# The RWKV-7 recurrence of a two-layer encoder: its products issued chunk by chunk in one fixed order, and the dense operands moved to multiples of 128 bytes

## Chip, cores and metric

The kernel runs on 1 core of one Trainium2 chip. The metric is the time of one execution on the device in microseconds (us). For the kernel before, three runs are shown; the profile is of one further execution, which the hardware profiler recorded.

## What is computed

The reference is an encoder trunk of two layers over 1024 positions of width 1024, all in float32. Layer 0 mixes positions with a gated block and trailing means, layer 1 with RWKV-7; a SwiGLU feed-forward network (FFN) with 2816 hidden units follows each. The part that the change rewrites is the recurrence of layer 1, for 16 heads of size 64:

```python
def step(state, inp):
    r_t, w_t, k_t, v_t, a_t, b_t = inp
    sa = jnp.einsum('bhvk,bhk->bhv', state, a_t)
    state = (state * w_t[:, :, None, :] + sa[..., None] * b_t[:, :, None, :]
             + v_t[..., None] * k_t[:, :, None, :])
    return state, jnp.einsum('bhvk,bhk->bhv', state, r_t)

s0 = jnp.zeros((bsz, nh, n, n), jnp.float32)
_, ys = lax.scan(step, s0, xs)
```

Around it stand plain matrix products: `h @ w` for the mixers' projections and `(silu(hn @ w_gate) * (hn @ w_up)) @ w_down` for the FFN.

## The kernel before

**Dense products.** The sequence is worked in two halves of 512 positions (`h` = 0 and 1). Each operand of a dense product is split into a high and a low part in the type float32r (`split`, L126: a copy on ACT, a subtraction on DVE), and each product is three matmuls, high times high, high times low and low times high (`mm3`, L323 to L326), with a stationary block of 128 by 128 weights and a moving block of 128 by 512 activations. The built program has 9,152 matmuls with float32r operands, 9,120 of them on the full 128 by 128 array. Weights come by DMA on ACT's queue, three tiles ahead, in the order of a list that is written out beforehand (`push...`, `take`).

**Recurrence.** `recur(h, wp)` (L1125) turns each half into 8 chunks of 64 positions, 16 chunks in all. All of its products are plain float32 and small, and each runs on a part of the array: 64 by 64 tiles for the Gram products (L1175, into `gt`), the chunk's own part (L1221), the product with the state (L1144, `sm<-S,ar`), the solve (L1144, `sm<-Q,XT`) and the output from the old state (L1266); 128 by 64 for the new state (L1250) and the output from the chunk (L1275); 32 by 32 for the two products that complete the triangular inverse (L1191 and L1210); the full array for the transposes (L1203, and L1330 in `post`). In a trace each of these matmuls is two instructions. `prep(c)` loads a chunk (SP's queue) and makes everything that doesn't need the state; `chain(c)` carries the state: product with the state, `Q` on DVE (L1237), solve, `uv` on ACT and DVE (L1241, L1242), new state, two DVE operations (L1256, L1257), and the outputs `yp`; `post` normalizes two chunks and stores them. PSUM has three buffers `sm` for all of these products, three `mm` for the dense ones and one for `yp`.

**What sets the order.** `recur` is a generator that yields a cost after each group of products. `drive` (L712) runs an FFN generator, which yields after every 3 matmuls (an eighth of a unit), and steps `recur` beside it until the costs that it yielded make up `RATIO` = 3.0 times the FFN's units. Every step of `recur` is emitted at a priority raised by `AHEAD` = 300, and a scheduler then places the instructions of each engine. It may interleave the products of different groups, and does. The two recurrences stand beside the FFN of layer 0 (second half) and of layer 1 (first half), L1473 and L1522.

**Tiles.** Pools of tiles are stacked from both ends of the on-chip memory. Several small tiles lie ahead of the large ones, such as `onesd` (one float), `mhalf`, `vec2`, `hfv`, `xss`, `hlast`, `pct`, and their widths set the addresses of what follows.

Of the kernel before, what the change touches and what calls it, by code (L numbers as in the profile page):

```python
# [12 lines left out]
ALU = mybir.AluOpType  # L13
# [16 lines left out]
RATIO, AHEAD, INV, FINE = 3.0, 300, 5, 1  # L30
LOWRANK_AT, GATE_AT, MIX_AT = (5, 8), (7, 8), 2

# [4 lines left out]
def tile_trunk(  # L37
# [11 lines left out]

    def open_pool(**kw):  # L50
        es = ExitStack()
        return es.enter_context(tc.tile_pool(reuse_waits="tile", **kw)), es
# [5 lines left out]
    const = ctx.enter_context(tc.tile_pool(name="const", bufs=1, side="left"))  # L58
    wst = ctx.enter_context(tc.tile_pool(name="wst", bufs=3, side="left"))
# [6 lines left out]
    onesd = const.tile([P, 1], F32, name="onesd")  # L66
    pool.memset(onesd, 1.0 / D)
    mhalf = const.tile([P, 16], F32, name="mhalf")
# [5 lines left out]
    vec2 = const.tile([P, 8], F32, name="vec2")  # L74
    omv = const.tile([P, P], F32, name="omv")
    hfv = const.tile([P, 16], F32, name="hfv")
# [212 lines left out]
    nt = ctx.enter_context(tc.tile_pool(name="nt", bufs=1, side="left"))  # L289
# [58 lines left out]
    def norm_rows(ms, scale=1.0):  # L348

        rs = nt.tile([P, 4], F32, tag="nrs", bufs=2, name="nrs")  # L350
# [56 lines left out]
    xss = const.tile([P, 8], F32, name="xss")  # L407
# [334 lines left out]
    hlast = const.tile([P, KT, 1], F32, name="hlast")  # L742
# [44 lines left out]
    def project_gate(h, hn1, kp, xlp, ring):  # L787
# [52 lines left out]
        def side():  # L840
            yield from split_steps()
            yield from mix_steps(hn1, 5, xs, ring_tiles(ring), kp)
            xr = act_tiles(xlp, 1 + HT)
            yield from mix_steps(hn1, 0, keep["xr"], lambda k: [x[:, k, 0:HT] for x in xr], kp)
            yield from mix_steps(hn1, 2, keep["xk"], ring_tiles(ring), kp)
# [279 lines left out]
    def recur(h, wp):  # L1125

        def wt(tag, bufs, shape):
            return wp.tile(shape, F32, tag=tag, bufs=bufs, name=tag)
# [10 lines left out]
        S = [state_d]  # L1139

        def prod(o, lhs, rhs):
            for p in range(8):
                for r in range(2):
                    pe.matmul(o[rows[r], p, :], lhs(r, p), rhs(r, p), start=True, stop=True)  # L1144
                if p == 3:
                    yield 0.7

        def prep(c):
# [18 lines left out]
            yield 0.2  # L1167
            gt = wt("gt", 2, [P, 8, 2, P])
            for q in range(2):
                og = [pst("sm").rearrange("p (a b) -> p a b", b=P) for _ in range(2)]  # L1170
                for j in range(4):
                    p = q * 4 + j
                    for b in range(2):
                        for r in range(2):
                            pe.matmul(  # L1175
                                og[r][rows[b], j, :], bk[rows[r], p, b, :],
                                ar[rows[r], p].rearrange("p a b -> p (a b)"), start=True, stop=True,
                            )
                    if j == 1:
                        yield 0.9  # L1180
                for r in range(2):
                    dve.tensor_tensor(
                        out=gt[:, q * 4 : q * 4 + 4, r, :], in0=og[r], in1=bc(gm.unsqueeze(1), [P, 4, P]), op=ALU.mult
                    )
                yield 0.9

            ow = smt()
            for p in range(8):
                for r in range(2):
                    b0 = r * 64  # L1190
                    pe.matmul(  # L1191
# [6 lines left out]
            yield 0.9  # L1198
            bkt = wt("bkt", 1, [P, 8, P])
            for q in range(2):  # L1200
                o = pst("sm").rearrange("p (a b) -> p a b", b=P)
                for j in range(4):
                    pe.transpose(o[:, j, :], bk[:, q * 4 + j].rearrange("p a b -> p (a b)"), ident)  # L1203
                act.activation(bkt[:, q * 4 : q * 4 + 4, :], o, AF.Copy)  # L1204
                yield 0.5
            ox = smt()
            for p in range(8):
                for r in range(2):
                    b0 = r * 64
                    pe.matmul(  # L1210
# [5 lines left out]
            yield 0.9  # L1216

            ov = smt()
            for p in range(8):
                for r in range(2):  # L1220
                    pe.matmul(  # L1221
                        ov[rows[r], p, :], gt[rows[1 - r], p, r, 0:64], uv[rows[1 - r], p, r, :], start=True, stop=True
                    )
                if p == 3:
                    yield 0.7
            akv = wt("akv", 1, [P, 8, 64])
            act.activation(akv, ov, AF.Copy)
            C[c] = (ar, uv, gt, bkt, XT, akv)
            yield 0.7

        def chain(c):
            ar, uv, gt, bkt, XT, akv = C.pop(c)
            S0 = S[0]
# [4 lines left out]
            yield 0.7  # L1238
            ou = smt()
            yield from prod(ou, lambda r, p: XT[rows[r], p, :], lambda r, p: Q[rows[r], p, :])  # L1240
            act.activation(uv[rows[0], :, 0, :], ou[rows[0]], AF.Copy)  # L1241
            dve.tensor_copy(uv[rows[1], :, 1, :], ou[rows[1]])  # L1242
            yield 0.7
            cg = h * 8 + c
            if cg < NCH - 1:
                Sn = state_d if c == 7 else wt("S", 2, [P, 8, 64])
                os_ = smt()
                for p in range(8):
                    for r in range(2):
                        pe.matmul(  # L1250
                            os_[rows[r], p, :], bkt[:, p, r * 64 : r * 64 + 64], uv[:, p, r, :], start=True, stop=True
                        )
# [317 lines left out]
```

## Time and profile before

| | us |
|---|---|
| median of the three runs (2617.55 to 2632.25) | 2624.68 |
| the profiled execution, its own time | 2628.69 |
| its span, from first to last instruction | 2627.0 |
| mean granted TensorE clock in it | 0.979 |

PE is the engine of the matmuls (TensorE), PEld its weight loads, DVE, ACT and POOL the vector, scalar and GpSimd engines, SP the engine that issues most of the transfers. A matmul's row in the trace shows when it started and a modelled duration. Matmuls overlap, so the distance from start to start, here called the pitch, says what one of them costs. PEclk is the share of the TensorE clock that was granted.

### The profile page before, as it was taken

To read this page: it belongs to the slowest core of one execution; us is meant where nothing else is said; L and a number is where in the kernel's file an instruction comes from. 1 tells how busy PE (TensorE), PEld (TensorE's weight loads), DVE (VectorE), ACT (ScalarE), POOL (GpSimd) and SP (SyncE) were. 2 spreads that over 40 slices of the span, in tenths; PEclk is the share of its full clock that TensorE was granted. 3 is DMA by queue.
4 is the path that set the end of the run, shared out by engine and by line. 5 is a ranking of instruction groups with operands and counts; after the bars stand their busy time and mean duration, and the time that the engine had idled before them with its cause. 6 is when DMAs were issued, how large, how long until landed. Compare 5 with 4: busy or idle time off the path is not lost.

```text
span 2627.0 us, 37918 instructions
## 1 busy us (share of the span) xinstructions
PE 2552.5 (97%) x15735; PEld 2041.2 (78%) x15735; DVE 1403.4 (53%) x2118; ACT 892.0 (34%) x1335; POOL 300.1 (11%) x298
## 2 busy tenths in 40 slices
PE   8999999999989999999999899999999999999998
PEld 6788888888767778788877677777877778888887
DVE  5446544345956864455547846754445454534344
ACT  6233332233543432232324644332133323423223
POOL 0200000001223300011002323201011000100001
PEclk9999999999989999999999999989999999999999
DMA  5113343232364683443233465683443332423321
GB/s 173 48 59 94 120 139 102 73 120 93 96 178 121 160 240 98 115 132 104 78 113 129 134 165 127 175 225 86 106 136 97 121 112 80 145 76 110 103 88 57
DMA packets 434956, 310.69 MB, mean 118 GB/s; under 512 B 93216, under 2 KB 395424, under 8 KB 433760
## 3 DMA queue, kind: packets, MB, share of 16 engines
q10 hardware_dynamic: 297280, 210.53, 27.1%
q1 hardware_dynamic: 137504, 97.75, 13.4%
q8 instruction: 123, 2.02, 0.3%
q14 instruction: 49, 0.40, 0.1%
HBM read 254.68 MB, written 53.54 MB: 117 GB/s over the span
## 4 chain that ended last, share of the span: by engine, by line
PE 85%; DVE 7%; DMA 4%; issue 2%; ACT 1%; POOL 0%; ACTq 0%; SPq 0%; DVEq 0%; POOLq 0%
PE mm L324 22%; PE mm L325 22%; PE mm L326 22%; PE sm L1175 2%; PE sm L1221 1%; PE sm L1144 1%; DVE wlo L128 1%; PE sm L1203 1%; DVE mix L868 1%; PE sm L1210 1%; PE sm L1191 1%; PE yp L1266 1%; PE yp L1275 1%; PE sm L1250 1%; DMA raw<-y_d 1%
## 5 line engine op out<-in xcount | busy, mean ns | idle before, releaser
L325 PE MATMUL mm<-alo,whi 128*128 128x512 f32 x1952 | 783.3, 401 | 1.6 <-DVE alo L128 1.6
L324 PE MATMUL mm<-ahi,whi 128*128 128x512 f32 x1952 | 778.6, 400 | 6.1 <-DVE h L403 5.1
L326 PE MATMUL mm<-ahi,wlo 128*128 128x512 f32 x1952 | 774.3, 397 | 2.5 <-DVE wlo L128 2.5
L127 ACT ACTIVATE whi<-raw 128x1024 fp32r<-128x1024 f32 x288 | 303.9, 1056 | 781.9 <-PE mm L325 647.6
L128 DVE TENSOR_TENSOR wlo<-raw,whi 128x1024 fp32r<-128x1024 f32 x288 | 362.6, 1259 | 308.6 <-ACT whi L127 291.8
L324 PEld LDWEIGHTS mm<-ahi,whi 128*128 128x128 f32 x1952 | 370.7, 190 | 99.5 <-ACT xhi L872 4.3
L326 PEld LDWEIGHTS mm<-ahi,wlo 128*128 128x128 f32 x1952 | 370.2, 190 | 89.2 <-DVE wlo L128 3.4
L325 PEld LDWEIGHTS mm<-alo,whi 128*128 128x128 f32 x1952 | 370.1, 190 | 87.6 <-DVE alo L128 3.2
L324 PE MATMUL mm<-hidhi,wdhi 128*128 128x512 f32 x624 | 241.0, 395 | 5.9 <-ACT hidhi L652 4.2
L325 PE MATMUL mm<-hidlo,wdhi 128*128 128x512 f32 x624 | 244.7, 392 | 1.1 <-DVE hidlo L653 1.0
L326 PE MATMUL mm<-hidhi,wdlo 128*128 128x512 f32 x624 | 244.9, 392 | 0.0
L403 DVE TENSOR_TENSOR h<-h,mm 128x512 f32<-128x512 f32 x192 | 129.4, 686 | 181.1 <-PE mm L326 180.4
L127 ACT ACTIVATE wdhi<-raw 128x1024 fp32r<-128x1024 f32 x82 | 86.5, 1061 | 236.9 <-DMA raw<-in_ffn_w_down_dram 145.7
L649 DVE TENSOR_TENSOR sg<-sg,mm 128x512 f32<-128x512 f32 x88 | 60.3, 687 | 183.3 <-PE mm L326 182.8
L128 DVE TENSOR_TENSOR wdlo<-raw,wdhi 128x1024 fp32r<-128x1024 f32 x82 | 102.8, 1255 | 91.9 <-ACT wdhi L127 91.9
L324 PEld LDWEIGHTS mm<-hidhi,wdhi 128*128 128x128 f32 x624 | 117.1, 188 | 34.4 <-ACT hidhi L652 5.5
L325 PEld LDWEIGHTS mm<-hidlo,wdhi 128*128 128x128 f32 x624 | 117.4, 188 | 26.7 <-DVE hidlo L653 2.4
L326 PEld LDWEIGHTS mm<-hidhi,wdlo 128*128 128x128 f32 x624 | 117.4, 188 | 25.0 <-issue 0.2
L403 DVE TENSOR_TENSOR hA<-hA,mm 128x512 f32<-128x512 f32 x72 | 48.9, 686 | 74.5 <-PE mm L326 74.5
L329 POOL TENSOR_TENSOR nrs<-nrs,mhalf 128x4 f32<-128x4 f32 x8 | 10.0, 1245 | 614.2 <-DVE nrs L351 614.2
L324 PE MATMUL mm<-xhi,whi 128*128 128x512 f32 (+1 forms) x160 | 66.0, 413 | 4.2 <-ACT k L906 4.2
L1204 ACT ACTIVATE bkt<-sm 128x512 f32<-128x512 f32 x32 | 19.1, 597 | 138.1 <-PE sm L1203 121.5
(298 smaller groups left out, 3162.8 us busy)
## 6 DMA issues: line engine op xcount, KB each, us to landing
raw<-in_ffn_w_gate_dram ACTq DMA_DIRECT2D x88, 512.0 KB
raw<-in_ffn_w_up_dram ACTq DMA_DIRECT2D x88, 512.0 KB
raw<-in_ffn_w_down_dram ACTq DMA_DIRECT2D x88, 512.0 KB
raw<-in_ab_w_in_dram ACTq DMA_DIRECT2D x16, 512.0 KB
raw<-in_ab_w_out_dram ACTq DMA_DIRECT2D x16, 512.0 KB
raw<-in_rwkv_w_k_dram ACTq DMA_DIRECT2D x16, 512.0 KB
raw<-in_rwkv_w_r_dram ACTq DMA_DIRECT2D x16, 512.0 KB
ar_d<-ar SPq DMA_DIRECT2D x16, 512.0 KB
```

What stands on the lines that cost most here:

```text
L127: act.activation(hi, src, AF.Copy)
L128: (eng or dve).tensor_tensor(out=lo, in0=src, in1=hi.bitcast(F32), op=ALU.subtract)
L324: pe.matmul(o, whi, xhi, start=first, stop=False)
L325: pe.matmul(o, whi, xlo, start=False, stop=False)
L326: pe.matmul(o, wlo, xhi, start=False, stop=last)
L403: dve.tensor_tensor(out=H[h][:, m, :], in0=H[h][:, m, :], in1=o, op=ALU.add)
L649: dve.tensor_tensor(out=s, in0=s, in1=o, op=ALU.mult)
L868: dve.scalar_tensor_tensor(out=t, in0=hn1[:, k, 0:HT], scalar=col(c), in1=t, op0=ALU.mult, op1=ALU.add)
L1144: pe.matmul(o[rows[r], p, :], lhs(r, p), rhs(r, p), start=True, stop=True)
L1175: pe.matmul(og[r][rows[b], j, :], bk[rows[r], p, b, :], ar[rows[r], p].rearrange("p a b -> p (a b)"), start=True, stop=True,)
L1191: pe.matmul(ow[b0 + 32 : b0 + 64, p, 0:32], gt[b0 : b0 + 32, p, r, 32:64], x1[b0 : b0 + 32, p, :], start=True, stop=True, tile_position=(b ...
L1203: pe.transpose(o[:, j, :], bk[:, q * 4 + j].rearrange("p a b -> p (a b)"), ident)
```

## The change

Three things change; what is computed stays the same, and so do the number and the sizes of all matmuls.

1. **The recurrence in bursts.** `prep` and `chain` are replaced by `load`, `gram`, `flip_bk`, `below`, `below2`, `own` and `burst`. Every matmul and transpose of the recurrence goes through `ordered`, which issues it after the one before it, so that their order on PE is the written one, with all products of one tile size in a row. The preparation of chunk `c + 1` (two Gram groups, transposes, first triangular product) stands inside the burst of chunk `c`; its loads are issued one chunk earlier, and `akv` and the second triangular product follow at the start of the next burst. A burst yields 0.1 after each group, and 12 units in two halves after its end, with `post` between them for odd chunks. The output from the old state is moved ahead of the new state.
2. **`AHEAD`** is 450 in place of 300.
3. **Addresses.** `Lines` widens each tile of a dense pool to a multiple of 32 floats (128 bytes); five small tiles become columns of one tile of 64 floats, `hlast` too; the small `nrs` and `fss` move to a pool of their own, on the other side, padded with `rest`; and the split tile of `side` is read as a dense one of 512 columns rather than at a stride of 513.

```diff
-RATIO, AHEAD, INV, FINE = 3.0, 300, 5, 1
+RATIO, AHEAD, INV, FINE = 3.0, 450, 5, 1
...
+BURST = 12.0
...
+        def tile(self, shape, dt, **kw):
+            n = math.prod(shape[1:])
+            if n % 32 == 0:
+                return self.pl.tile(shape, dt, **kw)
+            t = self.pl.tile([shape[0], n + -n % 32], dt, **kw)[:, :n]
...
+    small = const.tile([P, 64], F32, name="small")
+    onesd, mhalf, vec2, hfv, xss = (small[:, a:b] for a, b in ((56, 57), (0, 16), (16, 24), (24, 40), (40, 48)))
...
+    ns = ctx.enter_context(tc.tile_pool(name="ns", bufs=1, side="right"))
+    ns.tile([P, 8], F32, name="rest")
...
+        def ordered(f, *args, **kw):
+            if last:
+                with tc.issue_after(last.pop()):
+                    i = f(*args, **kw)
+            else:
+                i = f(*args, **kw)
+            last.append(i.ins)
...
+        def burst(c, bkt, w1):
+            ar, _, uv, gt, _, XT = C[c]
+            cg, S0, more = h * 8 + c, S[0], c < 7
+            below2(c, w1)
+            akv = own(c)
             oq = smt()
-            yield from prod(oq, lambda r, p: ar[rows[r], p, 0, :], lambda r, p: S0[rows[r], p, :])
+            each(oq, lambda r, p: ar[rows[r], p, 0, :], lambda r, p: S0[rows[r], p, :])
             Q = wt("Q", 1, [P, 8, 64])
             dve.tensor_tensor(out=Q, in0=akv, in1=oq, op=ALU.add)
-            yield 0.7
+            yield 0.1
+            if more:
+                gram(c + 1, 0)
+                yield 0.1
             ou = smt()
...
+            if more:
+                gram(c + 1, 1)
+                yield 0.1
             if cg < NCH - 1:
...
+            if more:
+                bkt = flip_bk(c + 1)
+                if c < 6:
+                    load(c + 2)
+                yield 0.1
+                w1 = below(c + 1)
+                yield 0.1
+            return bkt, w1
...
+        load(0)
+        load(1)
+        yield 0.2
+        gram(0, 0)
+        yield 0.5
+        gram(0, 1)
+        yield 0.5
+        bkt = flip_bk(0)
+        w1 = below(0)
+        yield 2.0
         for c in range(8):
-            yield from chain(c)
-            if c < 7:
-                yield from prep(c + 1)
+            bkt, w1 = yield from burst(c, bkt, w1)
+            yield BURST / 2
             if c % 2 == 1:
                 yield from post(c // 2)
+            yield BURST / 2
```

On PE, before, at the start of one chunk of the first half: the output from the old state (`yp<-S,ar`), the second triangular product (32 by 32, `sm<-XT,w`) and the chunk's own part (`sm<-uv,gt`) stand like this:

```order
L1266 MATMUL yp<-S,ar 64x64 x8
L1210 MATMUL sm<-XT,w_7941 32x32
L1221 MATMUL sm<-uv,gt 64x64 x2
L1210 MATMUL sm<-XT,w_7941 32x32 x10
L1221 MATMUL sm<-uv,gt 64x64
L1210 MATMUL sm<-XT,w_7941 32x32
```

The last two kinds go on in turn, one product of each, eight more rows. On PE, after, the same place in the burst of the second chunk, behind seven dense matmuls (L1168 is the line of `mm`, through which all of them go):

```order
L1168 MATMUL sm<-ar,bk 64x128 x15
L1168 MATMUL sm<-Q,XT 64x64 x16
L1168 MATMUL yp<-S,ar 64x64 x16
L1168 MATMUL sm<-ar,bk 64x128 x16
L1168 MATMUL sm<-uv,bkt 64x64 x16
L1168 MATMUL yp<-uv,gt 64x64 x16
L1168 MATMUL sm<-ident,bk 128x128 x8
L1168 MATMUL sm<-XT,gt 32x32 x16
```

Each group is whole and the groups follow each other without dense matmuls between them. Counted over the two recurrences, neighbours on PE that run on different tile sizes were 580 and are 154; of these, changes between 64 by 64 and 32 by 32 were 228 and are 10, between 32 by 32 and the full array 184 and 58, between 64 by 64 and the full array 116 and 50, others 52 and 36. From the first to the last product of a recurrence there stood 843 and 845 dense matmuls; now 594 and 632.

On DVE, before, from the evacuation of the triangular product (`XT`) of one chunk to the first operation of its new state (L403, L649, L653 and L128 are the dense work's own):

```order
L1215 COPY XT<-sm 32x8x32
L1237 TENSOR_TENSOR Q<-akv,sm 128x512
L403 TENSOR_TENSOR h<-h,mm 128x512 x2
L1242 COPY uv<-sm 64x8x64
L649 TENSOR_TENSOR sg<-sg,mm 128x512
L128 TENSOR_TENSOR wlo<-raw,whi 128x1024
L653 TENSOR_TENSOR hidlo<-sg,hidhi 128x512
L1256 TENSOR_TENSOR Q<-S,sm 128x512
```

On DVE, after, the same stretch (with the buffers' numbers, since four rows mask the next chunk's Gram products, `gt<-sm,gm`):

```order
L1256 COPY XT_7063<-sm_7543 32x8x32
L1278 TENSOR_TENSOR Q_7598<-akv_7579,sm_7581 128x512
L423 TENSOR_TENSOR h_7037<-h_7037,mm_7949 128x512
L1215 TENSOR_TENSOR gt_7384<-sm_7603,gm_1945 128x4x128
L1215 TENSOR_TENSOR gt_7384<-sm_7604,gm_1945 128x4x128
L1286 COPY uv_7060<-sm_7623 64x8x64
L1215 TENSOR_TENSOR gt_7384<-sm_7658,gm_1945 128x4x128
L1215 TENSOR_TENSOR gt_7384<-sm_7659,gm_1945 128x4x128
L1307 TENSOR_TENSOR Q_7699<-S_7317,sm_7682 128x512
```

The maskings moved in between the steps that the state waits for: two stand ahead of `uv` and two ahead of the new state.

In the built program, the moving operand and the stationary block both start at a multiple of 128 bytes for 962 of the 9,152 float32r matmuls before, and for 9,062 after. The most frequent case before is a moving operand at 64 bytes past such a multiple and weights at one (4,468), as in the last FFN; aligned before are, for one, the output projection of layer 0's mixer for the second half, around 220 us.

More of the change, by code (lines that the diff above doesn't have):

```diff
@@ L741, in tile_trunk @@
     bon = const.tile([P, 16, 8], F32, name="bon")
-    hlast = const.tile([P, KT, 1], F32, name="hlast")
+    hlast = small[:, 48:56].unsqueeze(2)
     def c64(t):
@@ L1166, in prep, with gram, flip_bk, below @@
                 pool.memset(XT[b0 + 32 : b0 + 64, :, 0:32], 0.0)
-            yield 0.2
             gt = wt("gt", 2, [P, 8, 2, P])
+            C[c] = (ar, bk, uv, gt, x1, XT)
+        def gram(c, q):
+            ar, bk, _, gt, _, _ = C[c]
+            og = [pst("sm").rearrange("p (a b) -> p a b", b=P) for _ in range(2)]
+            for j in range(4):
+                p = q * 4 + j
+                for b in range(2):
+                    for r in range(2):
+                        mm(
+                            og[r][rows[b], j, :], bk[rows[r], p, b, :],
+                            ar[rows[r], p].rearrange("p a b -> p (a b)"), start=True, stop=True,
+                        )
+            for r in range(2):
+                dve.tensor_tensor(
+                    out=gt[:, q * 4 : q * 4 + 4, r, :], in0=og[r], in1=bc(gm.unsqueeze(1), [P, 4, P]), op=ALU.mult
+                )
+        def flip_bk(c):
+            bk = C[c][1]
+            bkt = wt("bkt", 1, [P, 8, P])
             for q in range(2):
-                og = [pst("sm").rearrange("p (a b) -> p a b", b=P) for _ in range(2)]
+                o = pst("sm").rearrange("p (a b) -> p a b", b=P)
                 for j in range(4):
[L1172 to L1185, printed above, removed]
+                    ordered(pe.transpose, o[:, j, :], bk[:, q * 4 + j].rearrange("p a b -> p (a b)"), ident)
+                act.activation(bkt[:, q * 4 : q * 4 + 4, :], o, AF.Copy)
+            return bkt
+        def below(c):
+            _, _, _, gt, x1, _ = C[c]
             ow = smt()
@@ L1197, in prep, with below2 @@
             dve.tensor_copy(w1[96:128], ow[96:128, :, 0:32])
[L1198 to L1205, printed above, removed]
+            return w1
+        def below2(c, w1):
+            XT = C[c][5]
             ox = smt()
@@ L1215, in prep, with own @@
             dve.tensor_copy(XT[64:96, :, 32:64], ox[64:96, :, 0:32])
-            yield 0.9
+        def own(c):
+            _, _, uv, gt, _, _ = C[c]
             ov = smt()
@@ L1242, in chain @@
             dve.tensor_copy(uv[rows[1], :, 1, :], ou[rows[1]])
[L1243 to L1252, printed above, removed]
-                    if p == 3:
-                        yield 0.7
-                tS = wt("Q", 1, [P, 8, 64])
-                dve.tensor_tensor(out=tS, in0=S0, in1=os_, op=ALU.add)
-                dve.tensor_tensor(out=Sn, in0=tS, in1=bc(pct[:, cg, :].unsqueeze(2), [P, 8, 64]), op=ALU.mult)
-                S[0] = Sn
-                yield 0.7
+            yield 0.1
```

88 lines of the change are left out of this document (45 added, 43 removed).

## Prediction

> **What bounds the kernel now.** I read the page first, for the engines' shares and the chain that ended last.
>
> ```profile
> span 2627.0 us, 37918 instructions
> PE 2552.5 (97%) x15735; PEld 2041.2 (78%) x15735; DVE 1403.4 (53%) x2118; ACT 892.0 (34%) x1335; POOL 300.1 (11%) x298
> PE 85%; DVE 7%; DMA 4%; issue 2%; ACT 1%; POOL 0%; ACTq 0%; SPq 0%; DVEq 0%; POOLq 0%
> ```
>
> PE is busy nearly throughout and is 85% of the chain. A busy PE says little by itself, since matmuls overlap; so the windows came next. Their columns are the window, its length, PE's busy time with the number of instructions, the granted clock, and DMA.
>
> ```profile
> 300.00:500.00 200.00, 200.00 (x872) 1.00 0.37 113
> 961.00:1299.00 338.00, 334.94 (x3501) 0.96 0.41 116
> 1738.00:2078.00 340.00, 337.94 (x3471) 0.96 0.41 113
> 2400.00:2500.00 100.00, 100.00 (x434) 1.00 0.32 95
> ```
>
> Pure dense stretches run at 200 us / 872 = 229.4 ns and 100 / 434 = 230.4 ns a matmul, with PE never idle. The two recurrences take 338 and 340 us. They hold 843 and 845 dense matmuls, by the program's order, which at 230 ns are 194 us each. So some 144 us in each, 288 in all, go to the recurrence's small products and to what lies between them. Last, the waits of PE: those of the recurrence's products are few.
>
> ```profile
> PE sm L1191 <- DMA XT<-xi_d: 2.9, 1, 2.9
> PE yp L1266 <- DMA ar<-ar_d: 2.6, 1, 2.6
> PE sm L1175 <- DMA bk<-bk_d: 2.1, 1, 2.1
> ```
>
> Each came once, at a start of a recurrence. The kernel is bound by PE's own stream, so a change of the order or the pitch on PE shows in the time.
>
> **Changes of tile size.** The timeline of PE (start, duration, group) shows three kinds.
>
> ```profile
> 1027.85 0.40 PE L324 MATMUL mm<-ahi,whi 128*128 128x512 f32 x1
> 1028.18 1.15 PE L1144 MATMUL sm<-Q,XT 64*64 64x64 f32 x32
> 1029.26 0.50 PE L325 MATMUL mm<-alo,whi 128*128 128x512 f32 x1
> 1029.60 0.40 PE L326 MATMUL mm<-ahi,wlo 128*128 128x512 f32 x1
> ...
> 1090.27 0.66 PE L1203 MATMUL sm<-ident,bk 128*128 128x128 f32 x4
> ...
> 1095.14 0.33 PE L1203 MATMUL sm<-ident,bk 128*128 128x128 f32 x1
> 1095.40 0.24 PE L1191 MATMUL sm<-XT,gt 32*32 32x32 f32 x2
> 1095.57 0.33 PE L1203 MATMUL sm<-ident,bk 128*128 128x128 f32 x1
> ...
> 1102.02 0.57 PE L1210 MATMUL sm<-XT,w 32*32 32x32 f32 x24
> 1102.51 0.32 PE L1221 MATMUL sm<-uv,gt 64*64 64x64 f32 x2
> 1102.77 0.24 PE L1210 MATMUL sm<-XT,w 32*32 32x32 f32 x2
> 1102.94 0.33 PE L1221 MATMUL sm<-uv,gt 64*64 64x64 f32 x2
> ```
>
> One row of the groups gives the modelled length of a single instruction, 221 ns:
>
> ```profile
> L1144 PE MATMUL sm<-Q,XT 64*64 64x64 f32 x512 | 18.4, 221 | 0.0
> ```
>
> - Dense to 64 by 64 and back: from 1027.85 to 1029.60 are 1.75 us, for two dense matmuls (0.46) and a group of 32 instructions. The group alone takes its 1.15 less the 0.22 of the last instruction, 0.93. The rest, 0.36, is two changes: 0.18 each.
> - 64 by 64 and 32 by 32 in turn: a period is 1102.94 - 1102.51 = 0.43 us. Two L1210 instructions in a run cost 2 x 0.02 (24 in 0.49, from 1102.02 to 1102.51), the two of L1221 start 0.10 apart (0.32 less 0.22). What is left, 0.28, is two changes: 0.14 each.
> - Transposes and 32 by 32 in turn: a period is 0.43 us too (1095.57 - 1095.14). Less 0.04 and the two instructions of a transpose at 0.11 (four take 0.66, one 0.33), it leaves 0.17, 0.09 for a change.
>
> The order counts 580 changes before and 154 after, 426 fewer. At 0.09 they are worth 38 us, at 0.14 60 us. I take **40 us**, near the low end: before, products of the same tile size but of different groups also interleave, which hid part of each other's pitch, and whole groups lose that.
>
> [...]
>
> **The clock in the recurrence.** The granted clock is 0.96 there. Windows almost without dense matmuls differ:
>
> ```profile
> 1060.00:1063.40 3.40, 3.40 (x61) 1.00 1.08 221
> 1063.40:1070.20 6.80, 6.80 (x50) 0.50 0.25 50
> 1087.30:1090.70 3.40, 3.40 (x92) 1.00 0.98 232
> ```
>
> In the first, 32 by 32 and 64 by 64 take turns, and the clock is half behind it; in the third the Gram products and those with the old state run back to back, and it stays full. Half clock at a mean of 0.96 is 8% of 338 us, 27 us in each recurrence, in which at most half the work is lost: 13 us. Part of it lies at the starts, which stay. With the turns gone I take **10 us** back in all, between none and 27.
>
> **Alignment.** Two dense stretches of the timeline, the first with all operands at multiples of 128 bytes, the second with the moving ones 64 bytes past:
>
> ```profile
> 219.91 0.39 PE L324 MATMUL mm<-ahi,whi 128*128 128x512 f32 x1
> ...
> 224.67 0.39 PE L324 MATMUL mm<-ahi,whi 128*128 128x512 f32 x1
> ...
> 2309.73 0.40 PE L326 MATMUL mm<-ahi,wlo 128*128 128x512 f32 x1
> ...
> 2314.63 0.39 PE L326 MATMUL mm<-ahi,wlo 128*128 128x512 f32 x1
> ```
>
> Each pair is 21 matmuls apart: 4.76 / 21 = 226.7 ns and 4.90 / 21 = 233.3 ns, at full clock both. Misaligned stretches vary: the means over the windows above are 229.4 and 230.4 ns, 2.7 to 3.7 ns over the aligned one. On 9,120 full matmuls that is 25 to 34 us. In stages where DVE and DMA are late (the 11% of the chain) PE would only wait longer, so I take the low end, **25 us**. The bound below is nothing, if the difference is not the addresses'.
>
> [...]
>
> **What the bursts add.** Within a burst no dense work hides the waits, so the evacuations must fit under the other products. Their durations, from the groups by line:
>
> ```profile
> L1182 DVE TENSOR_TENSOR gt<-sm,gm 128x512 f32<-128x512 f32 x64 | 41.6, 684 | 8.3 <-PE sm L1175 7.9
> L1241 ACT ACTIVATE uv<-sm 64x512 f32<-64x512 f32 x16 | 9.5, 592 | 64.2 <-PE sm L1144 64.0 <-issue 0.3
> L1242 DVE COPY uv<-sm 64x512 f32<-64x512 f32 x16 | 11.1, 695 | 24.7 <-ACT uv L1241 24.5
> L128 DVE TENSOR_TENSOR wlo<-raw,whi 128x1024 fp32r<-128x1024 f32 x286 | 360.7, 1261 | 302.0 <-ACT whi L127 285.2 <-DMA g_d<-epx 4.9 <-DMA raw<-in_rwkv_w_o_dram 4.7
> ```
>
> `Q`, an operation of the maskings' kind, has seven dense matmuls (1.6 us) and 15 Gram products over it. The tightest is `uv`: from the end of the first Gram group DVE does two maskings (1.37) and then the `uv` copy (0.70), 2.1 us. PE has until the new state: the solve and the old-state output, 0.93 each, and a second Gram group of as many instructions on twice the columns, 0.93 at least, 2.8 us. That is 0.7 us of slack, less what the starts of these operations take; a weight split of DVE (`wlo`, 1.26) in front turns it into 0.6 us of waiting or more. The second Gram group also needs the PSUM buffers of the first, which costs up to 0.4 us more. Over 16 bursts I take 0.5 each, **8 us**; the bounds are none and 1.5 each, 24 us.
>
> The loads move a chunk ahead. SP's queue still has `gch` and `vch` between them, and the load of `bk` waits for the transposes to free its one buffer, then has some 20 dense matmuls (4.6 us) and three groups of products before its Gram products; the waits above show no such load late past the start, so this costs nothing, or with the bursts' bound. ACT's weight splits are emitted behind the evacuations; three weight tiles are ready, 72 dense matmuls, so the dense work hides them. `AHEAD` acts only through the order, which is counted above.
>
> **The sum.** 2628.7 - 40 - 10 - 25 + 8 = 2561.7 for an execution like the profiled one, which lies 4 us above the median of the runs: **2560 us**.
>
> **Rivals.**
>
> - *The addresses don't matter* (12%): the pitch differs for another cause, such as what else the stages read. Then 2560 + 25 = 2585. For it: misaligned stretches differ among themselves too, 229.4 and 230.4 ns above against 233.3. Against it: the aligned stretch lies below all of them.
> - *The bursts wait* (10%): evacuations or loads late by 1.5 to 2 us in each burst, since DVE and ACT work in order and carry dense splits. Then 24 to 32 us come back: about 2582. For it, the two maskings before `uv` in DVE's order; against it, the slack above.
> - *The clock falls in the bursts* (6%), the case that ends slower. A burst is some 15 us with seven dense matmuls (144 / 8 = 18 a chunk, less 2.5 for the changes that go), more than four windows of 3.4 us. If small products count for too little, half the clock is granted behind each window. At half clock they take up to twice as long, 15 x 16 = 240 us at most; half of it, 120, gives 2680. It turns on how much passes in 3.4 us: 92 instructions kept the clock, 61 did not.
> - *The order doesn't pay* (5%): the changes are gone but the products' own pitch grows by as much. Then 2560 + 40 = 2600 and no more than a per cent gained.
>
> The forecast itself has 67%. A measurement of this kernel can tell about 0.5% (13 us) from no change.
>
> **Range and chances.** With all terms at their good ends (60, 14, 34, no waits) it is 2516; with 38, none, 10 and 24, 2600. Few of these ends meet, so 2530 to 2600: it holds the forecast, the rivals of addresses and waits, and leaves out the falling clock, part of the last and the far ends, 2 in 10. Faster by over 0.5%: the forecast, the first two rivals and the fourth make 0.94, less 0.05 for waits beyond their bound, 0.89. Those 0.05 are within 0.5%. Slower: the clock, 0.06.
>
> **What would show it.** In the profile after: dense windows at 227 ns a matmul (x440 in 100 us); recurrences, from first to last product, some 258 and 266 us (594 and 632 dense at 0.227, and 144 - 21); few half-clock windows within them; in the waits of PE, lines of the `sm` products on DVE or ACT below 10 us in sum. I am wrong if dense windows stay at 230, if PEclk in the recurrences is below 0.9, or if small products wait 20 us and more.

## The result, and the profile after

| | before | after |
|---|---|---|
| median of the runs, us | 2628.15 (4 runs, 2617.55 to 2632.25) | 2534.88 (4 runs, 2528.54 to 2537.24) |
| ratio after to before, 95% interval | | 0.9647 (0.9626 to 0.9669) |
| profiled execution: its own time, us | 2628.69 | 2537.24 |
| its span, us | 2627.0 | 2535.5 |
| mean granted TensorE clock | 0.979 | 0.981 |

The change makes the kernel 93 us faster between the medians and 91.5 between the two spans. The forecast had 67 (2628.7 to 2561.7). The direction, the range (2530 to 2600) and every term's sign held; the sum came out 25 us too small.

The page of the changed kernel: its span, its engines, and the chain that ended last.

```profile
span 2535.5 us, 37947 instructions
PE 2443.4 (96%) x15735; PEld 1985.9 (78%) x15735; DVE 1401.2 (55%) x2118; ACT 889.8 (35%) x1335; POOL 298.9 (12%) x298
PE 76%; DVE 10%; DMA 8%; ACT 2%; issue 2%; POOL 1%; ACTq 0%; SPq 0%; DVEq 0%; POOLq 0%
```

PE has as many instructions as before, on 109 us less of busy time, and it is still what bounds the kernel. Its share of the chain fell from 85% to 76%: DVE and DMA hold more of the path now. The windows (length, PE's busy time and number, PEld, DVE, ACT, POOL, granted clock, DMA) say where the time went. The second and third are the recurrences, from the first to the last product.

```profile
300.00:500.00 200.00, 200.00 (x878) 164.39 (x878) 85.13 (x99) 51.62 (x63) 4.43 (x4) 1.00 0.35 107
957.40:1207.00 249.60, 235.56 (x3252) 194.04 (x3251) 133.76 (x270) 77.43 (x154) 35.28 (x28) 0.97 0.48 131
1703.20:1948.50 245.30, 238.49 (x3256) 198.62 (x3257) 134.54 (x270) 80.70 (x157) 36.77 (x28) 0.98 0.49 138
2300.00:2400.00 100.00, 100.00 (x443) 82.79 (x442) 40.57 (x47) 26.19 (x32) 0.00 (x0) 1.00 0.32 96
```

Dense stretches hold 878 matmuls in 200 us where 872 stood, and 443 in 100 where 434 stood. The recurrences take 249.5 and 245.2 us, where 258 and 266 were forecast. Taking 0.2275 us for each dense matmul between their first and last product leaves for the small ones, with all that lies between:

| us | first recurrence | second | sum |
|---|---|---|---|
| before | 337.6 - 843 x 0.2275 = 145.9 | 339.7 - 845 x 0.2275 = 147.4 | 293.3 |
| after | 249.5 - 594 x 0.2275 = 114.3 | 245.2 - 632 x 0.2275 = 101.5 | 215.8 |

So 77.5 of the 91.5 us come from the recurrences. Some 5 of them are the dense matmuls' own pitch: with the mean pitches that the next section gives, 0.2305 us before and 0.2280 after, the sums are 288 and 215, 73 us apart. This is how a burst looks in the timeline of PE (start, duration, group):

```profile
1106.35 1.15 PE L1168 MATMUL sm<-uv,bkt 128*64 128x64 f32 x32
1107.33 1.10 PE L1168 MATMUL yp<-uv,gt 128*64 128x64 f32 x32
1108.37 1.09 PE L1168 MATMUL sm<-ident,bk 128*128 128x128 f32 x8
...
1115.70 0.69 PE L1168 MATMUL sm<-XT,w 32*32 32x32 f32 x32
1116.32 0.97 PE L1168 MATMUL sm<-uv,gt 64*64 64x64 f32 x26
...
1118.07 0.38 PE L1168 MATMUL sm<-ar,bk 64*64 64x128 f32 x2
```

A group of 16 products takes 0.62 us on 32 by 32 (1116.32 - 1115.70, with the change behind it), and two groups on 64 by 64 take 1.75 (1118.07 - 1116.32). Last, the waits of PE (for what, us in total, times, longest), first recurrence and second:

```profile
PE sm L1168 <- DVE gt L1215: 7.0, 4, 4.0
PE sm L1168 <- DVE XT L1256: 5.0, 1, 5.0
PE sm L1168 <- POOL ysb L1368: 1.4, 1, 1.4
...
PE sm L1168 <- DVE gt L1215: 3.4, 2, 2.9
PE sm L1168 <- DVE XT L1256: 2.8, 1, 2.8
PE sm L1170 <- DMA bk<-bk_d: 1.3, 1, 1.3
...
PE sm L1168 <- DVE Q L1278: 0.2, 1, 0.2
```

They sum to 21 us, against 7.6 before, and most lie in the first two chunks: behind 1000 us the first recurrence has 3.8 us of them, and behind 1740 us the second has the 0.2. The timeline of all engines at the longest of them, with the idle time ahead of an instruction and what ended it in brackets:

```profile
989.09 1.06 ACT L145 ACTIVATE whi<-raw 128x1024 fp32r<-128x1024 f32 x1 [4.04 <-DMA raw<-in_ffn_w_up_dram]
990.18 1.23 DVE L146 TENSOR_TENSOR wlo<-raw,whi 128x1024 fp32r<-128x1024 f32 x1 [5.72 <-ACT whi L145]
991.43 0.69 DVE L423 TENSOR_TENSOR h<-h,mm 128x512 f32<-128x512 f32 x1
...
991.86 0.37 ACT L1255 ACTIVATE XT<-sm 32x256 f32<-32x256 f32 x1 [1.71 <-DVE wlo L146]
...
992.26 0.42 DVE L1256 COPY XT<-sm 32x256 f32<-32x256 f32 x1
...
992.74 0.69 PE L1168 MATMUL sm<-ar,bk 64*64 64x128 f32 x2 [5.04 <-DVE XT L1256]
```

Read from the bottom: PE waits for the copy of `XT`, which stands on DVE behind a weight split `wlo` and an update of `h`; `wlo` waits for ACT's `whi`, which waited for weights from DRAM. The evacuations are not slow (0.37 and 0.42 us); they stand in line behind a split whose weights are late.

### The profile page after: what moved, and what is told of

The parts are those of the page before. It is cut to its first block, busy times and chain, and to the rows that moved or that the text cites. A ratio compares the mean times of both kernels' runs of the same rounds, so it can differ in the third digit from the quotient of the medians.

```text
span 2535.5 us, 37947 instructions
## 1 busy us (share of the span) xinstructions
PE 2443.4 (96%) x15735; PEld 1985.9 (78%) x15735; DVE 1401.2 (55%) x2118; ACT 889.8 (35%) x1335; POOL 298.9 (12%) x298
## 3 DMA queue, kind: packets, MB, share of 16 engines
q8 instruction: 123, 2.02, 0.3%
## 4 chain that ended last, share of the span: by engine, by line
PE 76%; DVE 10%; DMA 8%; ACT 2%; issue 2%; POOL 1%; ACTq 0%; SPq 0%; DVEq 0%; POOLq 0%
PE mm L345 21%; PE mm L344 21%; PE mm L346 21%; PE sm L1168 5%; DVE wlo L146 2%; DMA raw<-in_ffn_w_up_dram 2%; PE yp L1168 1%; DVE mix L887 1%; DVE it L1117 1%; DMA lnw<-in_rwkv_ln_w_dram 1%; DMA raw<-in_ffn_w_down_dram 1%; DVE xi L1122 1%; DMA raw<-n_d 1%; ACT whi L145 1%; DMA raw<-y_d 1%
## 5 line engine op out<-in xcount | busy, mean ns | idle before, releaser
L345 PE MATMUL mm<-alo,whi 128*128 128x512 f32 x1952 | 773.8, 396 | 1.6 <-DVE alo L146 1.6
L344 PE MATMUL mm<-ahi,whi 128*128 128x512 f32 x1952 | 769.0, 395 | 5.0 <-DVE h L423 4.0
L349 POOL TENSOR_TENSOR nrs<-nrs,small 128x4 f32<-128x4 f32 x8 | 10.0, 1246 | 627.3 <-DVE nrs L371 627.3
L672 DVE TENSOR_TENSOR hidlo<-sg,hidhi 128x512 fp32r<-128x512 f32 x88 | 65.7, 746 | 3.8 <-ACT hidhi L671 3.7
```

What stands on the lines that cost most here:

```text
L344: pe.matmul(o, whi, xhi, start=first, stop=False)
L345: pe.matmul(o, whi, xlo, start=False, stop=False)
L672: dve.tensor_tensor(out=lo, in0=s, in1=hi.bitcast(F32), op=ALU.subtract)
```

## The experiments

All ratios are to the kernel before, run beside each kernel; the changed kernel's is 0.9647. Where kernels are compared in us, their medians come from different sets of runs, in which the median of the kernel before was 2625.2, 2627.4, 2627.3 and, with the changed kernel, 2628.2 us. The main theory after the result: the terms of the forecast are the right ones and act separately, and the changes of tile size are worth more than the 0.09 us that the sum used. The rivals: the pitch of the dense matmuls fell because of the order; or something else of the burst, its loads or its headstart, carries the gain.

**Addresses alone.** Part 3 of the diff on the kernel before, its recurrence and `AHEAD` untouched.

> The addresses alone: the kernel before with Lines, the small tile and the dense reading of the split tile, and its recurrence and AHEAD as before. Its order on PE is that of before (580 changes of tile size), 9,062 of its float32r matmuls are aligned. Theory (the terms are separate: the pitch of dense matmuls fell from 230.5 to 228.0 ns between the two profiles, 2.5 ns on some 9,100): 23 us faster than before, ratio 0.991, dense stretches near 440 matmuls in 100 us. Rival one (the pitch fell because the bursts leave long dense stretches alone, not because of the addresses): within 5 us of before. Rival two (the addresses also quicken the recurrence's small products): 40 us faster or more.

Measured: 0.9948 (0.9930 to 0.9966), 14 us faster.

```profile
300.00:500.00 200.00, 200.00 (x876) 164.03 (x875) 91.41 (x110) 54.73 (x68) 4.43 (x4) 1.00 0.37 114
2300.00:2400.00 100.00, 100.00 (x443) 82.79 (x441) 40.93 (x48) 25.92 (x32) 0.00 (x0) 1.00 0.32 101
```

The pitch did all that was expected (443 in 100 us): averaged over all neighbouring dense matmuls that start less than 0.3 us apart, it is 228.1 ns, as in the changed kernel (228.0), against 230.5 before. So rival one is refuted, and rival two, 40 us or more, with it. But 2.4 ns on some 9,000 pairs are 22 us, and 14 were gained. Its ten executions ran at a mean granted clock of 0.9765, those of before at 0.9795; the last section prices that at some 5 us. Its profiled execution had a clock of 0.981, and its span, 2600.4 us, is 26.6 shorter than that of before.

**The order alone.** Bursts and `AHEAD` = 450, with part 3 left out.

> The order alone: bursts and AHEAD 450 as in the changed kernel, all tiles where they are before (962 aligned). Its order on PE is that of the changed kernel, 154 changes of tile size. Theory (terms separate): the 91.5 us between the profiles less 23 for the addresses, 68 us faster than before, ratio 0.974, dense stretches near 434 in 100 us. Rival one (pitch from the long stretches): 85 to 91 us faster. Rival two (addresses quicken the small products too): 50 us faster or less.

Measured: 0.9699 (0.9666 to 0.9731), 80 us faster (79 by the ratio). Dense stretches are those of before:

```profile
300.00:500.00 200.00, 200.00 (x873) 163.43 (x872) 84.72 (x98) 50.81 (x62) 4.44 (x4) 1.00 0.35 109
2300.00:2400.00 100.00, 100.00 (x434) 81.22 (x433) 40.25 (x46) 24.76 (x30) 0.00 (x0) 1.00 0.31 95
```

The mean pitch is 230.5 ns. 14 and 79 make 93, the whole change, so the two parts look separate, with intervals of 5 and 9 us to either side of them; and the order has more than the 42 us (40 + 10 - 8) that the forecast gave it.

**The order left free.** `ordered` only issues:

```diff
         def ordered(f, *args, **kw):
-            if last:
-                with tc.issue_after(last.pop()):
-                    i = f(*args, **kw)
-            else:
-                i = f(*args, **kw)
-            last.append(i.ins)
+            f(*args, **kw)
```

> The changed kernel without the fixed order: the same bursts, loads and addresses, but each product placed by the scheduler, which interleaves groups again, 583 changes of tile size. Theory (the changes of tile size carry the order's gain, 429 of them at 0.16 us): 65 to 70 us slower than the changed kernel, about 23 us faster than before, ratio to before 0.991. Rival (the loads a chunk earlier and the preparation inside the burst carry it, not the sequence on PE): within 20 us of the changed kernel, ratio to before below 0.975.

Measured: 1.0037 (1.0018 to 1.0056), 10 us slower than before and 100 slower than the changed kernel. The loads and the preparation inside the burst are worth nothing by themselves: without the fixed sequence the whole gain is gone, and more. The theory's 65 to 70 us is too small again: it has no term for the 390 products that, by the order, stand without a neighbour on the other half of the rows (3 in the changed kernel), nor for the clock, which was 0.973 on the mean over its ten executions and 0.982 in the changed kernel.

**`AHEAD` back at 300.**

> The changed kernel with AHEAD 300, its value before. By the program's order 267 changes of tile size instead of 154, since dense matmuls stand inside the bursts again. Theory (0.16 us for each change): 113 more changes, 18 us slower than the changed kernel, ratio to before 0.972. Rival one (dense matmuls inside a burst hide waits, which is worth as much): within 6 us of the changed kernel. Rival two (less headstart makes the evacuations and loads late): 30 us slower or more.

Measured: 0.9781 (0.9746 to 0.9816), 30 us slower than the changed kernel between the medians. By the order, 99 of the 113 further changes are between 64 by 64 and the full array; at 0.18 us for those and 0.09 for the rest they make 19 us. PE's waits of `sm` products sum to 26 us in the two recurrences, 5 more. By the order 58 products have no partner on the other half of the rows, some 3 us at the prices found below, and the mean clock was 0.980, not 0.982, some 4 us by the last section's line. These make 31; the headstart's main effect is that the bursts stay whole.

**Changes put back, one of each in turn, and two of each.** In both, the second triangular product (32 by 32) and the chunk's own part (64 by 64) alternate; in the second kernel the two products `r` = 0 and 1 of a head pair stay neighbours.

```diff
-            below2(c, w1)
-            akv = own(c)
+            akv = below2(c, w1)
...
             for p in range(8):
                 for r in range(2):
                     b0 = r * 64
                     mm(
                         ox[b0 : b0 + 32, p, 0:32], w1[b0 + 32 : b0 + 64, p, :], XT[b0 + 32 : b0 + 64, p, 32:64],
                         start=True, stop=True, tile_position=(b0 + 32, b0),
                     )
+                    mm(ov[rows[r], p, :], gt[rows[1 - r], p, r, 0:64], uv[rows[1 - r], p, r, :], start=True, stop=True)
```

> The changed kernel with changes of tile size put back on purpose: the 16 products of below2 (32 by 32) and the 16 of own (64 by 64) are issued one of each in turn, 633 changes of tile size instead of 154, all else as it was. In the trace of before such a turn has a period of 0.43 us, and whole groups take 0.50 / 16 = 0.03 and 0.93 / 16 = 0.06 a product in the changed kernel: 0.34 us for two changes, 0.17 each. Theory (changes are paid at the price that the timeline shows, nothing hides them): 479 x 0.17 = 81 us slower than the changed kernel, about as slow as before (ratio 0.99 to 1.00). Rival one (a change costs the 0.09 of the prediction's sum): 43 us slower, ratio 0.981. Rival two (the loss is hidden, since later work waits for other things): under 15 us slower, ratio 0.970 or less.

> As the one with one of each in turn, but two and two: the two products of a head pair, which lie on different halves of the rows, stay side by side. 380 changes of tile size, 226 more than the changed kernel. Theory A (the change of tile size alone costs 0.17): 38 us slower than the changed kernel, ratio to before 0.979, half the loss of the one with single turns. Theory B (part of the 0.17 is that a product runs alone instead of beside its partner on the other half of the rows, 0.10 us instead of 0.06 for one of 64 by 64, and the change itself costs 0.14): 32 us slower or less, and in the timeline a period of two and two is at most 0.04 us longer than one of one and one (0.43).

Measured: one of each 1.0122 (1.0087 to 1.0158), 125 us slower than the changed kernel; two of each 0.9750 (0.9718 to 0.9782), 28 us slower. Half as many changes cost a fifth. The timeline of PE, one of each:

```profile
1128.02 0.32 PE L1168 MATMUL sm<-uv,gt 64*64 64x64 f32 x2
1128.28 0.24 PE L1168 MATMUL sm<-XT,w 32*32 32x32 f32 x2
1128.45 0.33 PE L1168 MATMUL sm<-uv,gt 64*64 64x64 f32 x2
1128.70 0.24 PE L1168 MATMUL sm<-XT,w 32*32 32x32 f32 x2
...
1131.23 0.47 PE L1168 MATMUL sm<-uv,gt 64*64 64x64 f32 x2
1131.63 0.31 PE L1168 MATMUL sm<-XT,w 32*32 32x32 f32 x2
1131.87 0.47 PE L1168 MATMUL sm<-uv,gt 64*64 64x64 f32 x2
```

and two of each:

```profile
1100.59 0.33 PE L1168 MATMUL sm<-uv,gt 64*64 64x64 f32 x4
1100.85 0.25 PE L1168 MATMUL sm<-XT,w 32*32 32x32 f32 x4
1101.03 0.33 PE L1168 MATMUL sm<-uv,gt 64*64 64x64 f32 x4
```

A period of two and two takes 1101.03 - 1100.59 = 0.44 us, one of one and one 1128.45 - 1128.02 = 0.43, for half the products. The second product of a pair rides along. In whole groups a pair takes 0.06 us on 32 by 32 and 0.12 on 64 by 64 (16 products in 0.50 and 0.93), so the two changes in the 0.44 are worth 0.26, 0.13 each; the 226 further changes make 29 us, and 28 were measured. The remaining 0.17 of the 0.43 are two products without a partner, 0.08 more than the same two cost beside one: some 0.05 for the one of 64 by 64 and 0.03 for the one of 32 by 32. This is theory B, with both prices.

One of each loses more than 479 x 0.17 = 81 us: the clock fell too, to a mean of 0.959 against 0.982, by the last section's line some 41 us. In the windows of that kernel, the two recurrences and then the turns above:

```profile
959.40:1281.80 322.40, 317.98 (x3342) 256.16 (x3342) 141.84 (x278) 86.08 (x163) 35.66 (x28) 0.89 0.38 108
1753.40:2070.60 317.20, 309.43 (x3268) 248.79 (x3268) 136.80 (x272) 82.00 (x158) 35.50 (x28) 0.88 0.39 107
...
1127.40:1130.60 3.20, 3.20 (x29) 2.15 (x27) 0.27 (x1) 0.00 (x0) 0.00 (x0) 0.99 0.37 108
1130.60:1137.40 6.80, 6.80 (x60) 5.16 (x60) 0.42 (x1) 0.91 (x2) 0.00 (x0) 0.50 0.12 35
```

From 1130.6 on half the clock is granted, and the period goes to 0.64 us (1131.87 - 1131.23). PE is busy throughout, with 29 instructions in the 3.2 us before and 60 in these 6.8: the clock fell, as the prediction's rival had it; what makes it fall is not shown. Whole groups did not bring it about. In the changed kernel, once the first 40 us of each recurrence are over, the clock is halved only twice, from 1055.1 and from 1092.6 us on, and both times PE had waited: of the 3.4 us before, it was busy for 1.21 and 1.36.

**Two groups of one tile size in turn.** The solve and the output from the old state, both 64 by 64, alternate product by product:

```diff
-            each(ou, lambda r, p: XT[rows[r], p, :], lambda r, p: Q[rows[r], p, :])
...
             for p in range(8):
                 for r in range(2):
+                    mm(ou[rows[r], p, :], XT[rows[r], p, :], Q[rows[r], p, :], start=True, stop=True)
                     mm(
                         yp[rows[r], p, :], ar[rows[r], p, 1, :], S0[rows[r], p, :], start=p == 0, stop=False,
                         skip_group_check=True,
                     )
```

> The changed kernel with two groups of the same tile size in turn: the solve and the output from the old state (both 64 by 64), first one of the solve and then one of the output on the same half of the rows. 174 changes of tile size instead of 154. Theory A (what the prediction assumed: products of one tile size but of different groups hide part of each other's pitch): the two groups take less than their 1.86 us, say 1.4, 7 us faster than the changed kernel, less 3 for the changes. Theory B (what makes products quick is that neighbours lie on different halves of the rows; in turn they lose that): 32 products a chunk at 0.10 instead of 0.06 us, 16 x 32 x 0.04 = 20 us slower and 3 for the changes, ratio to before 0.974. Theory C (neither): within 5 us of the changed kernel, ratio 0.965 to 0.967. In all of them uv can be up to 0.9 us later in a chunk, which may add waits, and would be seen as waits of PE on uv.

Measured: 0.9676 (0.9638 to 0.9713), 9 us slower than the changed kernel between the medians, with intervals that overlap. Theory A, the prediction's assumption, is refuted for these two groups by the timeline: from the first start of their products to the last are 2.02 us in 12 of the 16 chunks, in this kernel as in the changed one. Nothing was hidden. One chunk of each, from the first product of the solve to the bulk of the second Gram group, this kernel first (2.03 us) and then the changed one (2.02):

```profile
1103.28 0.27 PE L1168 MATMUL sm<-Q,XT 64*64 64x64 f32 x2
...
1105.31 1.09 PE L1168 MATMUL sm<-ar,bk 64*64 64x128 f32 x27
...
1103.31 0.27 PE L1168 MATMUL sm<-Q,XT 64*64 64x64 f32 x2
...
1105.33 1.09 PE L1168 MATMUL sm<-ar,bk 64*64 64x128 f32 x27
```

Theory B's condition did not arise, which I had overlooked: in this order a product of one group stands beside one of the other group on the other half of the rows, and by the program's order only 11 products lack a partner. The waits say what the 9 us may be: those of the recurrence's products sum to 28 us against 21, since the later `uv` brings waits that the changed kernel doesn't have; 20 more changes make some 3 us.

```profile
PE sm L1168 <- DVE Q L1306: 3.0, 1, 3.0
...
PE sm L1168 <- DVE uv L1296: 2.1, 1, 2.1
...
PE sm L1168 <- DVE Q L1306: 3.2, 1, 3.2
```

**Partners taken away, no change added.** The loops over `p` and `r` of three groups on 64 by 64 are exchanged:

```diff
-            for p in range(8):
-                for r in range(2):
+            for r in range(2):
+                for p in range(8):
                     mm(o[rows[r], p, :], lhs(r, p), rhs(r, p), start=True, stop=True)
```

> The changed kernel with the two loops of three groups exchanged (the chunk's own part, the product with the state, the solve): first the eight products of the lower half of the rows, then the eight of the upper half. By the program's order 628 products of 64 by 64 then have no neighbour of their tile size on the other half of the rows, in place of none, and the changes of tile size are 150 in place of 154. Theory (a product beside its partner rides along: in the runs with turns one product of 64 by 64 alone takes 106 ns and a pair 114): 628 x 0.05 = 31 us slower than the changed kernel, ratio to before 0.976, and a row of such products at a pitch near 0.10 us each in the timeline. Rival (the partner does not matter, all of the order's gain was the changes of tile size): within 5 us of the changed kernel, ratio 0.963 to 0.967.

Measured: 0.9737 (0.9722 to 0.9752), 22 us slower between the medians, though its executions ran at a slightly higher clock (0.983 on the mean). The two groups that took 1.75 us in the changed kernel:

```profile
1121.49 1.72 PE L1168 MATMUL sm<-uv,gt 64*64 64x64 f32 x29
...
1124.51 0.32 PE L1168 MATMUL sm<-ar,bk 64*64 64x128 f32 x1
```

They take 3.02 (1124.51 - 1121.49): 1.27 more for 32 products, 0.04 each. The theory holds, with 0.04 in place of its 0.05 us, and no change of tile size lies between these products.

**Operands moved off again.** A pad of 64 bytes ahead of the activations, and one at the start of the left side, which moves weights and activations:

```diff
+    nt.pl.tile([P, 16], F32, name="off")
...
+    const.pl.tile([P, 16], F32, name="off")
```

> The changed kernel with one pad of 64 bytes ahead of the activations on the left side: 5,766 float32r matmuls have a moving operand 64 bytes past a multiple of 128 and a stationary block at one, 3,104 stay aligned; the order is the changed kernel's. Theory (the address sets the pitch): 231 to 233 ns where it is off, as in the kernel before in its last network, 4 to 5 ns more on 5,766, some 25 us slower at the same clock, some 6 of it given back by the clock; ratio 0.969 to 0.974. Rival (the pitch is not the address's): 227 to 228 ns throughout, ratio 0.965.

> The changed kernel with one pad of 64 bytes at the start of the left side: 5,958 float32r matmuls have both operands 64 bytes past a multiple of 128, 2,032 stay aligned. Theory A (each operand has to be at a multiple of 128): a pitch of 231 ns or more on those, ratio 0.969 to 0.974. Theory B (what matters is that both lie alike, since the few such matmuls of before ran at 227.1 ns): 227 to 228 ns, ratio 0.964 to 0.966.

Measured: 0.9681 (0.9660 to 0.9701) and 0.9668 (0.9651 to 0.9684), 9 and 6 us slower than the changed kernel: the addresses cost something, but less than expected. The windows, first of the pad ahead of the activations:

```profile
300.00:500.00 200.00, 200.00 (x874) 163.68 (x873) 86.14 (x100) 51.49 (x63) 4.44 (x4) 1.00 0.36 110
2300.00:2400.00 100.00, 100.00 (x439) 82.22 (x438) 41.55 (x48) 24.74 (x30) 0.00 (x0) 1.00 0.33 99
```

and of both moved:

```profile
300.00:500.00 200.00, 200.00 (x867) 162.38 (x866) 84.98 (x99) 51.18 (x63) 4.44 (x4) 1.00 0.35 107
2300.00:2400.00 100.00, 100.00 (x443) 82.70 (x442) 42.15 (x49) 25.54 (x32) 0.00 (x0) 1.00 0.32 98
```

Neither theory survives as stated. With both operands 64 bytes off, one stage is the slowest of all kernels (867 in 200 us), while another runs as fast as if all were aligned (443), and in both two thirds of the matmuls have that same offset. So the offset from a multiple of 128 bytes alone does not set the pitch. Sorting the neighbouring dense matmuls of each trace by the offsets that the built program gives their two operands says more. In the kernel before, the mean is 227.6 ns with both at a multiple, 227.0 and 228.2 with both off by the same 64 or 96 bytes, and 231.6, 233.0 and 235.8 where the two differ (moving 64 past, stationary 64 past, moving 96 past): there a matmul was slow when its operands lay unlike. But with the pad ahead of the activations the 64-past ones run at 229.9, and with both operands moved the like ones at 229.5. What else in the addresses counts was not tried further and stays open.

**An attempt at a faster version.** The loads of the second chunk move behind the first triangular product of the first:

```diff
         load(0)
-        load(1)
         yield 0.2
...
         w1 = below(0)
+        load(1)
         yield 2.0
```

> The changed kernel with the loads of the second chunk issued after the first triangular product of the first chunk instead of right behind the first chunk's loads. In the changed kernel PE waits some 20 us at the starts of the two recurrences, mostly for DVE operations that stand behind a weight split whose weights land late. Theory (the weights are late because two chunks' loads share the DMA engines with them): 5 to 10 us faster than the changed kernel, ratio 0.961 to 0.963. Rival (the loads aren't it, the splits wait for other reasons, such as the mixers' last stores): within 3 us, ratio 0.965, and the same waits at the starts.

Measured: 0.9638 (0.9605 to 0.9670), 1.3 us below the changed kernel between the medians, which is within the noise. In this run's trace the waits of the recurrences' products sum to 19 us, against 21 without the edit, most of them still at the starts. Nothing gained that can be told; the rival stands. With the triangular product also moved ahead of the transposes:

```diff
+                w1 = below(c + 1)
+                yield 0.1
                 bkt = flip_bk(c + 1)
                 if c < 6:
                     load(c + 2)
-                yield 0.1
-                w1 = below(c + 1)
                 yield 0.1
```

> An attempt at a faster version: the changed kernel with the second chunk's loads behind the first triangular product, as in the run before, and with the triangular product (32 by 32) ahead of the transposes, whose tile size is that of the dense matmuls behind them: 140 changes of tile size in place of 154. Theory (0.13 us a change, and the 1 to 2 us that the loads' place gave): 3 to 4 us faster than the changed kernel, ratio 0.963; a difference this small is at the edge of what five rounds can tell. Rival (the triangular product now waits for the maskings of the second Gram group, which DVE finishes just before): 16 x 0.3 = 5 us slower, ratio 0.966 or more.

Measured: 0.9659 (0.9641 to 0.9678), no faster. Its waits of PE for the Gram maskings are 8.9 and 9.8 us in the two recurrences, against 7.0 and 3.4, while those for `XT` fell from 5.0 and 2.8 to 3.1 and 0.3; the sum of the waits is 24 us against 21, which takes the 2 us that 14 changes are worth. No version faster than the changed kernel was found.

## Why the prediction was right, and where its sum was off

The terms, as the forecast put them and as the runs size them:

| term, us gained | forecast | sized by the runs |
|---|---|---|
| changes of tile size, 426 fewer | 40 | 54 |
| products that get a partner back | 0 | 22 |
| clock | 10 | 7 |
| alignment | 25 | 22 by the pitch |
| waits | -8 | -13 |
| sum | 67 | 92 (the spans say 91.5) |

That 92 meets 91.5 so closely is partly luck: the mean clocks have three digits, so that term alone is known to some 3 us, and the partners are 18 us at 0.04. The same terms do fit the profiled executions of the two parts. For the order alone, 54 and 22, less 11 for the waits (18.6 us against 7.6), and 14 of clock (55 - 2544.9 x 0.016) make 79, and the two spans are 82.1 apart. For the addresses alone, 22 and 6 of clock make 28, and the two spans are 26.6 apart. The range held by 5 us at its fast end, and one of the four executions, 2528.54, lies outside it.

- **Changes.** The step that failed is "I take **40 us**, near the low end: before, products of the same tile size but of different groups also interleave, which hid part of each other's pitch, and whole groups lose that". Nothing was hidden, as the run with two groups of one size in turn shows for a pair of them. The prediction's own three prices, with these counts, make some 56 us. By the order, the 426 are 218 between 64 by 64 and 32 by 32, 126 between 32 by 32 and the full array, 66 between 64 by 64 and the full array, and 16 others; at 0.13, 0.09, 0.18 and 0.13 they are worth 54 us. Only the 0.13 was tested by a run of its own; the other two are the prediction's.
- **Partners.** The interleaving did the opposite of hiding. By the order, 344 products of 64 by 64 and 156 of 32 by 32 stood without a neighbour on the other half of the rows before, and 3 in all after. At 0.05 and 0.03 that is 22 us, a term that the prediction put at nothing. Its rows had it: it took 0.10 us for the two instructions of the lone product of 64 by 64 out of the 0.43 us period, and 0.93 for a whole group of 16 such products, which is 0.06 each, but it didn't count the 0.04 between them as a gain of whole groups.
- **Clock.** Each span times the clock not granted is 2627.0 x 0.021 = 55 us before and 2535.5 x 0.019 = 48 after. Within the recurrences more came back (0.96 became 0.97 and 0.98 over shorter stretches, 27 us became 12); elsewhere some was lost. Of those 12 most stand at the starts, where PE waits: the granted clock is 0.88 from 957.4 to 1000 and from 1703.2 to 1740 us, 0.98 and 1.00 in the rest.
- **Alignment.** The pitch fell by 2.5 ns, near the low end of the 2.7 to 3.7 that the prediction took. Of the resulting 22 us the medians show 14 alone, at a lower clock, and 13 on top of the order, with an interval of 10 to either side. The rival "the addresses don't matter" is refuted; that multiples of 128 bytes are the reason isn't shown, and the like operands off a multiple, at 227.0 and 228.2 ns, speak against it.
- **Waits.** The 0.5 us a burst for `uv` and the PSUM buffers did not come: the slack held. The 13 us lie at the starts instead, where evacuations stand behind weight splits. The bound that the prediction set itself, lines on DVE and ACT below 10 us in sum, was missed with 18. With 21 us of waits in all, one of its signs of being wrong, "if small products wait 20 us and more", came about: the prediction looked for the waits inside the bursts and put 8 us there, and they came at the starts. The rival "the bursts wait" named late evacuations, which did come, but in the first chunks only and not in each burst.
- **The rivals.** "The order doesn't pay" is refuted by the order alone, which has 79 us. "The clock falls in the bursts" did not happen (0.97 and 0.98 in the two recurrences), but with single turns the clock did fall, to 0.89 and 0.88 there.

## What to carry to other kernels

Issue small products in whole groups of one tile size, with neighbours on different halves of the rows: a change of tile size costs 0.09 to 0.18 us here (0.13 by a run of its own, the ends by timeline alone), and a product of 64 by 64 without a partner 0.04 to 0.05 us. When a period of a turn is taken apart, price the products at what they cost in that turn, and look for what could have run beside them. A scheduler that is free to interleave can undo a good emission order entirely, so count changes and missing partners in the built order, not in the source.

## What was not expected of the hardware

- Most of the spread between executions of one kernel goes with the granted clock. Over the 33 runs of the kernel before that were made beside the experiments, the mean clock goes from 0.972 (2641.57 us) to 0.984 (2613.64 us); a line through them has 1.8 us for each 0.001, with a correlation of -0.88. Kernels differ in their mean clock as well: 0.9765 for the addresses alone, 0.959 with single turns. Why aligned addresses without bursts run at a lower clock than before is not shown.
- A busy PE did not hold the clock. With single turns PE is busy for all of 3.2 us (29 instructions), and the next 6.8 us are granted half the clock (60 instructions), while the turns go on.
- The pitch of a dense matmul depends on where its operands lie: in one stage by 2% (443 against 434 matmuls in 100 us, the order of the instructions unchanged), at full clock and with PE never idle. What makes it differ is not shown.
